# Stick-breaking attention without the weights: running products times differences of values, a second gate in pairs, sums of x from the last scores on

## The chip, the cores and the metric

One core of one Trainium2 chip runs the whole layer in one launch. The metric is the device time of an execution in microseconds; the kernel before takes 768.82 us (median of 3 runs, 767.13 to 770.05). PE is the matrix engine, DVE the vector engine, ACT the scalar engine, POOL the fourth compute engine, SP the queue that starts most DMAs; ACT and POOL can start DMAs too. Everything is float32; a product of matrices is made of three passes of rounded parts ("high" times "high", "high" times "low", "low" times "high").

## The reference

```python
u = x @ w_in + b_in                       # x: (1024, 1024)
q, k, v, z_att, glu_a, glu_b, z_conv, g_att, g_conv = split(u)
# 8 heads of 64: beta[t,s] = sigmoid(q_t.k_s / 8), s < t
# A[t,s] = beta[t,s] * prod_{s<j<t} (1 - beta[t,j]);  att[t] = sum_s A[t,s] v[s]
att_branch  = (att * silu(z_att)) @ w_att_proj
c = causal_depthwise_conv(glu_a * sigmoid(glu_b), conv_w) + conv_b       # 31 taps
conv_branch = (silu(layer_norm(c)) * silu(z_conv)) @ w_conv_proj + b_conv_proj
merged = sigmoid(g_att) * att_branch + sigmoid(g_conv) * conv_branch
out = layer_norm(2 ** 0.25 * x + merged @ w_out)
```

## The kernel before, in words

All engines' instructions are written out by a planner: `Timeline` (L65) keeps a modelled clock for each engine, generators yield their next operation with a priority, and the main loop (L1203) puts on PE, in this order of preference, waiting small products, a step of attention (`Attention.step`, L827), or the next group of a "dense" product (`run_dense`, L307). The result is one fixed order for each engine; at run time an engine takes its instructions strictly in that order and each waits for the semaphores of what it reads or overwrites. Tiles come from pools: 43 blocks of 128x1024 (`blk`), 8 half tiles of 128x512 (`hf`), 8 PSUM banks (`bank`).

The stages, in order of time. First the values, v = x times its weights, for eight blocks of 128 tokens (`vps`, L1145). DVE adds the bias (`vraw`, L1158), ACT rounds (`v`, L1160), DVE takes the rest (L1161), so that each head has 64 columns of high and 64 of low parts. Then attention, with dense products between its steps: queries and keys (`qk_item`), the inputs of the convolution (`glu_item`), the gate z_att (`zatt_item`, L1061), and the first parts P1, P2 of "pairs" (`p12_item`). Attention goes by head and by 256 queries (`Unit`): scores (`zps`, L734, L735), two sigmoids on ACT, f = 1 - beta (L742) and b = beta (L743), a running product of f on DVE (L749, from right to left, started by the unit matrix in `eyez`), the weight b times the next product (L752), transposes on PE (`tps`, L767), rounding (`wth`, `wtl`), and the product with v (`pvps`, L790). High and low halves of that product are added by ACT (L805) and DVE (L806) into `att`. When both heads of an `att` tile are done its gate is computed from PSUM (`ev_zatt`, L430) and the product is kept in DRAM (`keep`).

Then the pairs (`run_pairs`, L1023): two groups of 128 output columns are computed in seven half products P1 to P7 in place of eight, from sums and differences of x (`make_t`, L873) and of the weights (`make_s`). Before, there are ten pairs, for g_att, g_conv and z_conv. While the last pair runs, `split_att` (L456) reads `att` back and rounds it into `ach` and `acl`. Then the two projections (`ev_a`, `ev_c`), the output product (`yps`) and the last layer norm. The convolution's multiplications fill DVE at the lowest priority.

Weights come by SP into `wr`, ACT rounds them into `wh`, and the rest `wl` is made by POOL, DVE, or a DMA of POOL's that adds the weights to their negated rounding (L241, L242).

Of the kernel before, what the change touches and what calls it, by code (L numbers as in the profile page):

```python
# [14 lines left out]
P = 128  # L15
# [19 lines left out]

N_BLK, N_HF, N_RAW, N_SPL = 43, 8, 2, 5

N_F, N_W = 3, 5
# [23 lines left out]
W_LAND = 3000  # L62


class Timeline:  # L65
# [96 lines left out]
def layer_kernel(ctx: ExitStack, tc, xT, x, wv, wd, wa, wc, wo, vec, bv, lng, lnb, cst, out):  # L162
# [70 lines left out]
    def split_weight(wh, wl, r, src, direct, then):  # L233
# [21 lines left out]
    def feed(loads=1 << 30):  # L255
        while True:
# [21 lines left out]
            if i < min(loads, len(pieces)):  # L278
# [99 lines left out]
    za_left = [2] * NC  # L378
# [44 lines left out]
    def silu_pre(ps, ci, name):  # L423
        s = hfp.tile([P, HALF], F32, name="sg" + name, tag="hf")
        yield act(0, s, ps, AF.Sigmoid, bias=vcol(ci))
        yield vstt(0, s, ps, vcol(ci), s, ALU.add, ALU.mult)
        drop("ps")
        return s

    def ev_zatt(p):  # L430
        def f(half, cols, ps):
            def g():
                s = yield from silu_pre(ps, ZATT0 + p, f"za{p}{half}")
                a = att[p][:, cols]
                e = yield vtt(1, a, a, s, ALU.mult)
                drop("hf")
                za_left[p] -= 1
                if za_left[p] == 0:
                    keep(("att", p), att[p])

            tl.spawn(g(), tl.t + 165)
        return f

    def keep(key, src, cols=slice(0, S)):

        if key not in kept:
            kept[key] = dram.tile([P, S], F32, name="_".join(map(str, key)), tag="_".join(map(str, key)))
        nc.sync.dma_start(kept[key][:, cols], src)
        n_kept[key] = n_kept.get(key, 0) + 1

    def back(key, name):
        t = blk(name)
        nc.sync.dma_start(t, kept[key])
        return t

    def split_att(p):  # L456
# [61 lines left out]
    def make_cc(i):  # L518

        while n_kept.get(("c", ZCONV0 + i), 0) < 2:  # L520
            yield tl.now + 200
        z = back(("c", ZCONV0 + i), f"zs{i}")
        yield tl.now + 3500
# [184 lines left out]
    slots = {"f": 0, "w": 0}  # L708

    def alloc_unit(u):  # L710
        n = u.nslots
        ft = [blk(f"f{u.h}{u.m}{i}") for i in range(n)]
        bt = [blk(f"b{u.h}{u.m}{i}") for i in range(n)]
        slots["f"] += n
        slots["w"] += n
        if n == 1:
            u.f = [ft[0][:, 0:HALF], ft[0][:, HALF:S]]
            u.w = [bt[0][:, 0:HALF], bt[0][:, HALF:S]]
        else:
            u.f, u.w = [t[:, :] for t in ft], [t[:, :] for t in bt]  # L720
        for tb in range(2):

            last = P * (2 * u.m + tb + 1) - 1
            nc.gpsimd.memset(u.w[tb][:, last:last + 1], 0.0)
            tl.cost("G", tl.t, 0)

    def emit_z(u):
# [10 lines left out]
        f, w = u.f[tb], u.w[tb]  # L738
        c2 = min(c1, n - 1)

        def g():
            yield act(0, f[:, c0:c1], ps[:, :c1 - c0], AF.Sigmoid, n=c1 - c0, scale=-SCALE)  # L742
            yield act(0, w[:, c0:c2], ps[:, :c2 - c0], AF.Sigmoid, n=c1 - c0, scale=SCALE)  # L743
# [5 lines left out]
            yield ("V", 2, n, lambda: nc.vector.tensor_tensor_scan(  # L749
                f[:, 0:n][:, ::-1], f[:, 0:n][:, ::-1], eyez[:, S - n:S][:, ::-1], 0.0, op0=ALU.mult,  # L750
                op1=ALU.max), {"per": 2.083})
            u.ready[tb] = yield vtt(1, w[:, 0:n - 1], w[:, 0:n - 1], f[:, 1:n], ALU.mult, n)  # L752
            if u.nslots == 2 or u.ready[1 - tb] is not None:
                slots["f"] -= 1
# [3 lines left out]
    def emit_t(u):  # L758
# [22 lines left out]
    def emit_pv(u, i, wh, wl):  # L781
# [13 lines left out]
        if i == 0:  # L795
            p = h // 2
            if att[p] is None:
                att[p] = blk(f"att{p}")
            tmp = hf(f"pvt{h}{m}")
            r0 = (h % 2) * DH  # L800
            dst = att[p][r0:r0 + DH, m * 256:(m + 1) * 256].rearrange("p (b t) -> p b t", b=2)[:, ::-1, :]
            two = lambda ap: ap.rearrange("p (b t) -> p b t", b=2)

            def g():
                yield act(0, tmp[0:DH, 0:256], u.ps[DH:P, 0:256], n=256)  # L805
                yield vtt(0, dst, two(u.ps[0:DH, 0:256]), two(tmp[0:DH, 0:256]), ALU.add, 256)  # L806
                drop("ps")
                drop("hf")
                heads_cnt[h] += 1
                if heads_cnt[h] == 4:  # L810
                    heads_done[p] += 1
                    if all(n == 2 for n in heads_done):
                        flags["att"] = True
                        tl.spawn(make_t(0), tl.now)
                        tl.spawn(make_t(1), tl.now)
# [4 lines left out]
    class Attention:  # L820
# [6 lines left out]
        def step(self):  # L827

            now = tl.t
            if self.pvq and self.pvq[0][0] is not None and self.pvq[0][0] <= now - GUARD and \  # L830
# [3 lines left out]
            if self.zd and live["hf"] <= N_HF - 2 and live["ps"] < 7:  # L834
                u = self.zd[0]
                if all(r is not None and r <= now - GUARD for r in u.ready):
                    self.pvq.append(emit_t(u))
                    if not u.t:
                        self.zd.popleft()
                        slots["w"] -= u.nslots  # L840
                    return True
            if self.cur is None and self.wait:
                u = self.wait[0]
                if qk_ready[u.h] <= now and slots["w"] + u.nslots <= N_W and slots["f"] + u.nslots <= N_F:
                    self.cur = self.wait.popleft()
                    alloc_unit(u)
            if self.cur is not None and live["ps"] < 6:
                emit_z(self.cur)
                if not self.cur.z:
                    self.zd.append(self.cur)  # L850
                    self.cur = None
                return True
# [9 lines left out]
    pairs = [(c, c + 1) for c in (*range(GA0, GA0 + NK, 2), *range(GC0, GC0 + NK, 2), *range(ZCONV0, ZCONV0 + NC, 2))]  # L862
# [5 lines left out]
    t12, t34, first = {}, {}, {}  # L868
    source, split_done = {}, {}
# [3 lines left out]
    def make_t(k):  # L873
# [4 lines left out]
        yield tl.now + 4500  # L878
# [4 lines left out]
        yield vtt(1, b[:, hi_], rb[:, lo_], a[:, hi_], ALU.subtract)  # L883
        for t, r, name in ((t12, a, "ta"), (t34, b, "tb")):
# [4 lines left out]
        if k + 2 < NK // 2:  # L889
# [503 lines left out]
```

## Time and profile before

| what | us |
|---|---|
| median of 3 runs (lowest, highest) | 768.82 (767.13, 770.05) |
| the profiled execution | 767.04 |
| its span, first to last instruction | 765.0 |
| PE, DVE, ACT, POOL busy | 748.2, 651.3, 379.7, 69.5 |
| granted TensorE clock, mean | 0.994 |

The span leaves 2.04 us outside it. A busy time counts a stretch once in which instructions of a group overlap; matmuls overlap, so what one costs is read from the distance of starts and not from its own duration.

### The profile page before, as it was taken

To read this page: it belongs to the slowest core of one execution; us is meant where nothing else is said; L and a number is where in the kernel's file an instruction comes from. 1 tells how busy PE (TensorE), PEld (TensorE's weight loads), DVE (VectorE), ACT (ScalarE), POOL (GpSimd) and SP (SyncE) were. 2 spreads that over 40 slices of the span, in tenths; PEclk is the share of its full clock that TensorE was granted. 3 is DMA by queue.
4 is the path that set the end of the run, shared out by engine and by line. 5 is a ranking of instruction groups with operands and counts; after the bars stand their busy time and mean duration, and the time that the engine had idled before them with its cause. 6 is when DMAs were issued, how large, how long until landed. Compare 5 with 4: busy or idle time off the path is not lost.

```text
span 765.0 us, 10211 instructions
## 1 busy us (share of the span) xinstructions
PE 748.2 (98%) x3622; PEld 625.4 (82%) x3622; DVE 651.3 (85%) x1006; ACT 379.7 (50%) x716; POOL 69.5 (9%) x132
## 2 busy tenths in 40 slices
PE   9999999999999999999999999999998999999995
PEld 7888888788888878888888888877786888888885
DVE  7554999999999999997999999999699859810985
ACT  2149965986388799844524433345472424200100
POOL 3311011101011011101100000000000023000000
PEclk9999999999999999999999999999999999999998
DMA  7525123412432224557725454453347876230052
GB/s 233 184 63 110 35 56 74 92 30 62 103 80 59 57 56 96 125 140 259 207 83 185 146 163 155 139 191 125 126 149 240 317 266 217 79 148 1 0 200 75
DMA packets 43394, 98.01 MB, mean 128 GB/s; under 512 B 4816, under 2 KB 5712, under 8 KB 43344
## 3 DMA queue, kind: packets, MB, share of 16 engines
q1 hardware_dynamic: 36864, 85.77, 33.5%
q0 software_dynamic: 6336, 11.54, 9.4%
q8 instruction: 28, 0.46, 0.3%
q14 instruction: 22, 0.18, 0.1%
q10 hardware_dynamic: 144, 0.07, 0.0%
HBM read 77.95 MB, written 19.40 MB: 127 GB/s over the span
## 4 chain that ended last, share of the span: by engine, by line
PE 58%; DVE 25%; ACT 9%; issue 6%; DMA 2%; SPq 0%; DVEq 0%; ACTq 0%
PE dps L203 11%; PE dps L198 11%; PE dps L199 11%; PE vps L1145 6%; DVE cacc L399 4%; PE yps L209 4%; PE yps L210 4%; PE yps L211 4%; PE pvps L790 3%; PE tps L767 3%; DVE cs L399 2%; DVE wl L396 2%; DVE c L396 2%; DVE cacc L396 2%; DVE u L396 2%
## 5 line engine op out<-in xcount | busy, mean ns | idle before, releaser
L198 PE MATMUL dps<-xh,wh 128*128 128x512 f32 x400 | 157.0, 393 | 0.0
L199 PE MATMUL dps<-xl,wh 128*128 128x512 f32 x400 | 156.0, 390 | 0.0
L203 PE MATMUL dps<-xh,wl 128*128 128x512 f32 x400 | 109.0, 391 | 0.0
L749 DVE TENSOR_TENSOR_SCAN f<-f,eyez 128x896 f32<-128x896 f32 (+3 forms) x64 | 85.0, 1343 | 5.1 <-ACT f L393 5.1
L235 ACT ACTIVATE wh<-wr 128x512 fp32r<-128x512 f32 x84 | 53.3, 634 | 72.4 <-DMA wr<-wv 25.5
L199 PEld LDWEIGHTS dps<-xl,wh 128*128 128x128 f32 x400 | 75.2, 188 | 14.2
L198 PEld LDWEIGHTS dps<-xh,wh 128*128 128x128 f32 x400 | 75.1, 188 | 14.3
L203 PEld LDWEIGHTS dps<-xh,wl 128*128 128x128 f32 x400 | 74.1, 188 | 14.6
L399 DVE SCALAR_TENSOR_TENSOR cacc<-cin,vecs,cacc 128x511 f32<-128x511 f32 (+14 forms) x116 | 82.4, 735 | 0.1
L242 POOL DMA_DIRECT2D wl<-wd x44 | 38.2, 868 | 271.7 <-ACT wl L241 240.8
L239 POOL TENSOR_TENSOR wl<-wr,wh 128x512 fp32r<-128x512 f32 x18 | 26.2, 1460 | 293.9 <-DVE wl L237 231.1
L210 PE MATMUL yps<-wol,mh 128*128 128x512 f32 (+1 forms) x136 | 51.2, 377 | 0.0
L211 PE MATMUL yps<-woh,ml 128*128 128x512 f32 (+1 forms) x136 | 51.2, 376 | 0.0
L209 PE MATMUL yps<-woh,mh 128*128 128x512 f32 (+1 forms) x136 | 51.2, 376 | 0.0
L396 DVE TENSOR_TENSOR wtl<-tps,wth 128x384 fp32r<-128x384 f32 (+1 forms) x80 | 46.7, 625 | 4.0 <-ACT wth L393 3.5
L399 DVE SCALAR_TENSOR_TENSOR xrow<-xrow,yps 128x512 f32<-128x512 f32 (+1 forms) x17 | 10.7, 653 | 43.0 <-PE yps L211 42.7
L393 ACT ACTIVATE f<-zps 128x384 f32<-128x384 f32 (+2 forms) x96 | 45.3, 515 | 3.8 <-PE zps L735 3.0
L393 ACT ACTIVATE wth<-tps 128x384 fp32r<-128x384 f32 (+1 forms) x80 | 40.2, 559 | 13.9 <-PE tps L767 13.2
L396 DVE TENSOR_TENSOR b<-b,f 128x895 f32<-128x895 f32 (+3 forms) x64 | 46.8, 743 | 0.3
L393 ACT ACTIVATE b<-zps 128x383 f32<-128x383 f32 (+2 forms) x96 | 46.2, 536 | 0.1
L399 DVE SCALAR_TENSOR_TENSOR cs<-cs,hs__77 128x511 f32<-128x511 f32 (+14 forms) x60 | 44.1, 735 | 0.1
L790 PE MATMUL pvps<-wtl,v 128*128 128x256 f32 (+1 forms) x160 | 39.7, 287 | 0.3 <-DVE wtl L396 0.2
(174 smaller groups left out, 1637.6 us busy)
## 6 DMA issues: line engine op xcount, KB each, us to landing
wr<-wd SPq DMA_DIRECT2D x60, 256.0 KB, 3.0
wl<-wd POOLq DMA_DIRECT2D x44, 256.0 KB, 4.6
rc<-wd SPq DMA_DIRECT2D x20, 512.0 KB, 5.6
c<-c SPq DMA_DIRECT2D x30, 256.0 KB, 3.1
ga<-c SPq DMA_DIRECT2D x8, 512.0 KB, 5.2
wor<-wo SPq DMA_DIRECT2D x16, 256.0 KB, 4.7
gc<-c SPq DMA_DIRECT2D x8, 512.0 KB, 6.3
xrow<-x SPq DMA_DIRECT2D x8, 512.0 KB, 5.8
```

The lines of the kernel that those rows point to most:

```text
L198: nc.tensor.matmul(ps, wh[:, kk], mh, start=first and kk is ks[0], stop=False)
L199: nc.tensor.matmul(ps, wh[:, kk], ml, start=False, stop=False)
L203: nc.tensor.matmul(ps, wl[:, kk], mh, start=False, stop=last and kk is ks[3])
L209: nc.tensor.matmul(ps, wh, mh, start=first, stop=False)
L210: nc.tensor.matmul(ps, wh, ml, start=False, stop=False)
L211: nc.tensor.matmul(ps, wl, mh, start=False, stop=last)
L235: yield "A", 1, HALF, lambda: nc.scalar.activation(wh, r, AF.Copy)
L393: return "A", u, n, (lambda: nc.scalar.activation(out, in_, func, **kw)), (BIAS if "bias" in kw else {})
L396: return "V", u, n, lambda: nc.vector.tensor_tensor(out, a, b, op=op)
L399: return "V", u, n, (lambda: nc.vector.scalar_tensor_tensor(out, a, s, b, op0, op1)), (PTR if ptr else {})
L749: yield ("V", 2, n, lambda: nc.vector.tensor_tensor_scan(f[:, 0:n][:, ::-1], f[:, 0:n][:, ::-1], eyez[:, S - n:S][:, ::-1], 0.0, op0=ALU.mult,
L790: nc.tensor.matmul(u.ps[:, 0:n], st, wt[:, jj * 256:jj * 256 + n], start=(i == m and jj == 0 and wt is wh), stop=(i == 0 and jj == 1 and w ...
```

## The change

Attention: with R[s] the running product of f from s to the query, a weight is R[s+1] - R[s], so the sum over s of weight times v[s] is v of the token before plus the sum of R[s] times (v[s-1] - v[s]). The second sigmoid, its tile and the multiplication go. For the differences, each block of v is copied one row down by a DMA of 127 rows from ACT's queue, with one more DMA for the row that comes from the block before; DVE subtracts. The leading v is transposed on PE (32 transposes) and copied by ACT into `att`, and each product of attention is then added by two DMAs of POOL's (high half, low half) in place of ACT's and DVE's addition. `pvps` waits until all v are there.

z_att is computed by two more pairs, kept in DRAM, and multiplied in `split_att`, which now reads eight blocks. The order of the dense products is a string; `make_t` starts when the last head's scores are out. DMAs take their turn on one modelled clock (`Timeline.dma`).

```diff
+T_AT = (7, 7)
-N_F, N_W = 3, 5
+N_F = 6
+ORDER = "q0 q1 g0 q2 g1 q3 p2 q4 q5 g2 p2 q6 q7 p2 g3 p3"
-W_LAND = 3000
+DMA_RATE, W_ACC = 250, 2.2
+    def dma(self, kb, when=None, weight=1.0):
+        when = max(self.now, self.t) if when is None else when
+        self.dma_free = max(self.dma_free, when) + weight * kb * 1024 / DMA_RATE
+        return self.dma_free + 2000
...
     def split_att(p):
+        yield from stored(("c", ZATT0 + p))
         a = back(("att", p), f"attb{p}")
-        yield tl.now + 3500
+        z = back(("c", ZATT0 + p), f"zab{p}")
+        yield landed[f"zab{p}"]
...
+            yield vtt(1, a[:, c], a[:, c], z[:, c], ALU.mult)
             yield act(0, ach[p][:, c], a[:, c])
             yield vtt(1, acl[p][:, c], a[:, c], f32(ach[p][:, c]), ALU.subtract)
...
             yield act(0, f[:, c0:c1], ps[:, :c1 - c0], AF.Sigmoid, n=c1 - c0, scale=-SCALE)
-            yield act(0, w[:, c0:c2], ps[:, :c2 - c0], AF.Sigmoid, n=c1 - c0, scale=SCALE)
...
-            u.ready[tb] = yield vtt(1, w[:, 0:n - 1], w[:, 0:n - 1], f[:, 1:n], ALU.mult, n)
...
-                yield act(0, tmp[0:DH, 0:256], u.ps[DH:P, 0:256], n=256)
-                yield vtt(0, dst, two(u.ps[0:DH, 0:256]), two(tmp[0:DH, 0:256]), ALU.add, 256)
+                yield act(0, two(tmp[:, 0:256])[:, ::-1, :], two(u.ps[:, 0:256]), n=256)
                 drop("ps")
+                for part in (slice(0, DH), slice(DH, P)):
+                    e = yield "G", 1, 0, (lambda part=part: nc.gpsimd.dma_start(dst, tmp[part, 0:256],
+                                                                                accum_op=ALU.add)), {"extra": 430}
+                    yield tl.dma(64, e, W_ACC) + 2000
...
-    pairs = [(c, c + 1) for c in (*range(GA0, GA0 + NK, 2), ...
+    pairs = [(c, c + 1) for c in (*range(ZATT0, ZATT0 + NC, 2), *range(GA0, GA0 + NK, 2), ...
...
     def ev_v(tb):
+        vraw[tb] = b = blk(f"vraw{tb}")
+        t, s = b[:, 0:HALF], b[:, HALF:S]
+        yield vtt(0, t, vps[tb], bvt, ALU.add)
+        drop("ps")
+        raw_there.add(tb)
+        while tb and tb - 1 not in raw_there:
             yield tl.now + 100
+        nc.scalar.dma_start(s[1:P, :], t[0:P - 1, :])
+        if tb:
+            nc.scalar.dma_start(s[0:1, :], vraw[tb - 1][P - 1:P, 0:HALF])
+        else:
+            nc.gpsimd.memset(s[0:1, :], 0.0)
+        got = []
+        def turn():
+            ps = bank("tps")
+            for p in range(NC):
+                nc.tensor.transpose(ps[:, p * P:(p + 1) * P], t[:, p * P:(p + 1) * P], ident)
+            tl.t += 4 * 109
+            got.append(ps)
+        yield turn
+        ps = got[0]
+        yield [act(1, att[p][:, tb * P:(tb + 1) * P], ps[:, p * P:(p + 1) * P], n=P) for p in range(NC)]
+        drop("ps")
+        yield tl.now + 1500
         vt[tb] = blk(f"v{tb}", F32R)
...
+        yield vtt(1, s, s, t, ALU.subtract)
+        yield "A", 0, HALF, lambda: nc.scalar.activation(v3[:, :, 0:DH], s3, AF.Copy)
+        yield "V", 1, HALF, lambda: nc.vector.tensor_tensor(v3[:, :, DH:P], s3, f32(v3[:, :, 0:DH]), op=ALU.subtract)
```

ACT's order before, just after the product for v (`vps`): its roundings of v, the weights of the next dense product, then the evacuation of head 0's queries and keys (`qhh`, `qll`, `ks`). What stands in brackets is what an instruction waits for; DMAHW0 to DMAHW7 are the eight marks that DMAs of SP and ACT take in turn.

```order
L1160 ACTIVATE v_458<-vraw_457 128x8x64 [waits DVE_49]
L1160 ACTIVATE v_464<-vraw_463 128x8x64 [waits DVE_49]
L235 ACTIVATE wh_408<-wr_406 128x512 [waits DMAHW7_49,PE_49,Pool_49]
L1160 ACTIVATE v_468<-vraw_467 128x8x64 [waits DVE_49]
L241 ACTIVATE wl_409<-wr_406 128x512
L1160 ACTIVATE v_487<-vraw_486 128x8x64 [waits DVE_49]
L235 ACTIVATE wh_473<-wr_471 128x512 [waits DMAHW0_49,PE_49,Pool_49]
L241 ACTIVATE wl_474<-wr_471 128x512
L393 ACTIVATE qhh_524<-dps,vecs 128x512 [waits PE_49]
```

ACT's order now, at the same place: the DMAs for the fifth to the eighth block of v and the first copies into `att`.

```order
L1146 DMA vraw_461<-vraw_461 127x512 [waits DMAHW0_49,DVE_49]
L1148 DMA vraw_461<-vraw_456 1x16x32 [waits DMAHW1_49]
L252 ACTIVATE wl_409<-wr_406 128x512
L1146 DMA vraw_467<-vraw_467 127x512 [waits DMAHW2_49,DVE_49]
L1148 DMA vraw_467<-vraw_461 1x16x32 [waits DMAHW4_49]
L1146 DMA vraw_472<-vraw_472 127x512 [waits DMAHW5_49,DVE_49]
L1148 DMA vraw_472<-vraw_467 1x16x32 [waits DMAHW6_49]
L1146 DMA vraw_486<-vraw_486 127x512 [waits DMAHW7_49,DVE_49]
L1148 DMA vraw_486<-vraw_472 1x16x32 [waits DMAHW0_49]
L403 ACTIVATE att_442<-tps 128x128 [waits PE_49]
L403 ACTIVATE att_443<-tps 128x128
```

The DMAs of all eight blocks now stand ahead of the copies into `att`, and the later ones wait for marks that the earlier ones hold; by the waits on DVE below, DMAHW0 is the first block's DMA, DMAHW1 the second's, DMAHW6 and DMAHW7 the fourth's.

DVE's order before, from the end of the roundings of v to the first running products (`f`) of head 0.

```order
L1161 TENSOR_TENSOR v_468<-vraw_467,v_468 128x8x64 [waits Activation_49]
L1161 TENSOR_TENSOR v_487<-vraw_486,v_487 128x8x64 [waits Activation_49]
L399 SCALAR_TENSOR_TENSOR qll_525<-dps,vecs,qhh_524 128x512 [waits Activation_49] x2
L749 SCALAR_TENSOR_TENSOR f_605<-f_605,eyez 128x896 [waits Activation_49]
L399 SCALAR_TENSOR_TENSOR qll_643<-dps,vecs,qhh_642 128x512 [waits Activation_49]
L396 TENSOR_TENSOR b_607<-b_607,f_605 128x895 [waits DVE_49]
L749 SCALAR_TENSOR_TENSOR f_606<-f_606,eyez 128x1024
```

DVE's order now, at the same place.

```order
L406 TENSOR_TENSOR vraw_456<-vraw_456 128x512 [waits DMAHW7_49,DMAHW6_49]
L406 TENSOR_TENSOR vraw_461<-vraw_461 128x512 [waits DMAHW1_49,DMAHW0_49]
L406 TENSOR_TENSOR vraw_467<-vraw_467 128x512 [waits DMAHW4_49,DMAHW2_49]
L406 TENSOR_TENSOR vraw_472<-vraw_472 128x512 [waits DMAHW6_49,DMAHW5_49]
L409 SCALAR_TENSOR_TENSOR qll_607<-dps,vecs,qhh_606 128x512 [waits Activation_49]
L406 TENSOR_TENSOR vraw_486<-vraw_486 128x512 [waits DMAHW7_49,DMAHW0_49]
L1171 TENSOR_TENSOR v_620<-vraw_472,v_620 128x8x64 [waits Activation_49]
L1171 TENSOR_TENSOR v_629<-vraw_486,v_629 128x8x64 [waits Activation_49]
L409 SCALAR_TENSOR_TENSOR qll_607<-dps,vecs,qhh_606 128x512 [waits Activation_49]
L736 SCALAR_TENSOR_TENSOR f_700<-f_700,eyez 128x896 [waits Activation_49]
L736 SCALAR_TENSOR_TENSOR f_701<-f_701,eyez 128x1024 [waits Activation_49]
```

The subtractions, each waiting for its block's two DMAs, now stand ahead of head 0's queries and keys (`qll`), and no multiplication stands behind a running product any more.

ACT's order now, a little later: from the rounding of the eighth block of v to the first tiles of head 0's queries and keys (`qhh`, `qll`, `ks`); four more rows stand before the first `f`.

```order
L1170 ACTIVATE v_629<-vraw_486 128x8x64 [waits DMAHW7_49,DMAHW0_49,DVE_49]
L403 ACTIVATE qhh_606<-qhh_606 64x512 [waits Activation_49]
L403 ACTIVATE qll_607<-qll_607 64x512 [waits Activation_49]
L403 ACTIVATE qhh_606<-dps,vecs 128x512 [waits PE_49]
L403 ACTIVATE ks_608<-qhh_606 64x512 [waits Activation_49]
L403 ACTIVATE ks_608<-qll_607 64x512 [waits DVE_49]
```

Head 0's tiles, which PE needs for the first scores, are finished behind the rounding of the last block of v; before, that rounding stood ahead of the first `qhh`.

## Rows read from the trace of the kernel before

**Rows 1.** The page: busy time of each engine (share of the span).

```profile
PE 748.2 (98%) x3622; PEld 625.4 (82%) x3622; DVE 651.3 (85%) x1006; ACT 379.7 (50%) x716; POOL 69.5 (9%) x132
```

**Rows 2.** Busy time by stretch: busy us of each engine, clock, DMA share, GB/s.

```profile
180.00:200.00 20.00, 20.00 (x113) 17.27 (x112) 19.81 (x31) 9.97 (x21) 1.73 (x2) 1.00 0.27 54
...
340.00:360.00 20.00, 20.00 (x90) 16.57 (x89) 15.44 (x23) 9.42 (x14) 1.96 (x3) 1.00 0.85 282
...
580.00:600.00 20.00, 17.48 (x67) 13.31 (x67) 15.56 (x24) 5.46 (x9) 0.00 (x0) 0.91 0.92 326
...
660.00:680.00 20.00, 20.00 (x90) 16.57 (x89) 10.39 (x16) 3.16 (x5) 0.00 (x0) 1.00 0.58 211
```

**Rows 3.** Waits of PE: us in total, times, longest us.

```profile
PE dps L199 <- DVE acl L396: 2.5, 3, 1.0
PE tps L767 <- DVE b L396: 1.6, 4, 0.5
PE sps L203 <- DVE wl L396: 1.3, 1, 1.3
```

**Rows 4.** Waits of PE's weight loads.

```profile
PEld tps L767 <- ACT ks L393: 1.9, 2, 0.9
PEld zps L735 <- ACT qll L393: 1.5, 5, 0.3
...
PEld tps L767 <- DVE b L396: 0.8, 2, 0.6
```

**Rows 5.** The chain in order of time: start us, us, what.

```profile
100.55 1.21 PE tps L767 x11
...
343.21 0.91 PE dps L203 x4
345.93 0.91 PE dps L203 x4
```

**Rows 6.** The page's costliest groups: count, busy us, mean ns, idle before.

```profile
L396 DVE TENSOR_TENSOR b<-b,f 128x895 f32<-128x895 f32 (+3 forms) x64 | 46.8, 743 | 0.3
L393 ACT ACTIVATE b<-zps 128x383 f32<-128x383 f32 (+2 forms) x96 | 46.2, 536 | 0.1
```

**Rows 7.** Groups of DVE and ACT by shape, same columns.

```profile
L396 DVE TENSOR_TENSOR u<-sps,u 128x512 f32<-128x512 f32 x30 | 20.4, 680 | 0.0
...
L396 DVE TENSOR_TENSOR att<-pvps,pvt 64x256 f32<-64x256 f32 x32 | 12.7, 407 | 1.4 <-ACT pvt L393 0.9
...
L393 ACT ACTIVATE qhh<-qhh 64x512 fp32r<-64x512 f32 x16 | 10.1, 631 | 0.4
...
L393 ACT ACTIVATE f<-zps 128x128 f32<-128x128 f32 x8 | 2.6, 320 | 0.0
```

**Rows 8.** The timeline after the product for v: start us, us, what.

```profile
45.01 4.77 DVE L396 TENSOR_TENSOR vraw<-vps,bvt 128x512 f32<-128x512 f32 x7 [12.25 <-PE vps L1145]
...
49.34 0.39 PE L1145 MATMUL vps<-wh,xl 128*128 128x512 f32 x1
...
64.98 0.33 PE L734 MATMUL zps<-ks,qhh 128*128 128x384 f32 x1
```

**Rows 9.** The page's DMA packets, and queues: packets, MB, share of 16 engines.

```profile
DMA packets 43394, 98.01 MB, mean 128 GB/s; under 512 B 4816, under 2 KB 5712, under 8 KB 43344
...
q1 hardware_dynamic: 36864, 85.77, 33.5%
q0 software_dynamic: 6336, 11.54, 9.4%
...
q10 hardware_dynamic: 144, 0.07, 0.0%
```

**Rows 10.** DMA issues: count, KB each, median us from issue to landing.

```profile
wl<-wd POOLq DMA_DIRECT2D x44, 256.0 KB, 4.6
...
p<-p SPq DMA_DIRECT2D x10, 256.0 KB, 3.0
...
attb<-att SPq DMA_DIRECT2D x4, 512.0 KB, 5.7
```

**Rows 11.** The timeline of PE after its waits for `acl`.

```profile
584.67 0.50 PE L199 MATMUL dps<-acl,wh 128*128 128x512 f32 x1 [1.00 <-DVE acl L396]
585.00 1.68 PE L203 MATMUL dps<-ach,wl 128*128 128x512 f32 x4
...
586.91 0.63 PE L199 MATMUL dps<-acl,wh 128*128 128x512 f32 x1
```

More of the change, by code (lines that the diff above doesn't have):

```diff
@@ L421, in ev_qk @@
         return f
[L423 to L442, printed above, removed]
+    landed = {}
     def keep(key, src, cols=slice(0, S)):
@@ L712, in alloc_unit @@
         ft = [blk(f"f{u.h}{u.m}{i}") for i in range(n)]
-        bt = [blk(f"b{u.h}{u.m}{i}") for i in range(n)]
         slots["f"] += n
[L715 to L725, printed above, removed]
+        u.f = [ft[0][:, 0:HALF], ft[0][:, HALF:S]] if n == 1 else [t[:, :] for t in ft]
     def emit_z(u):
@@ L811, in g @@
                     heads_done[p] += 1
+                    if heads_done[p] == 2:
+                        keep(("att", p), att[p])
                     if all(n == 2 for n in heads_done):
                         flags["att"] = True
-                        tl.spawn(make_t(0), tl.now)
-                        tl.spawn(make_t(1), tl.now)
+                        for k in {0, 1} - t_begun:
+                            tl.spawn(make_t(k), tl.now)
                         next_pair()
@@ L829, in step @@
             now = tl.t
-            if self.pvq and self.pvq[0][0] is not None and self.pvq[0][0] <= now - GUARD and \
+            if v_left[0] == 0 and self.pvq and self.pvq[0][0] is not None and self.pvq[0][0] <= now - GUARD and \
                     (self.pvq[0][1].ps is not None or live["ps"] < 7):
@@ L851, in step @@
                     self.cur = None
+                    for k, h in enumerate(T_AT):
+                        if k not in t_begun and heads_z_done(h):
+                            t_begun.add(k)
+                            tl.spawn(make_t(k), tl.t)
                 return True
             return False
-    pairs = [(c, c + 1) for c in (*range(GA0, GA0 + NK, 2), *range(GC0, GC0 + NK, 2), *range(ZCONV0, ZCONV0 + NC, 2))]
+    pairs = [(c, c + 1) for c in (*range(ZATT0, ZATT0 + NC, 2), *range(GA0, GA0 + NK, 2), *range(GC0, GC0 + NK, 2), *range(ZCONV0, ZCONV0 + NC, 2))]
     OPERAND = {"P3": "S4", "P4": "A22", "P5": "S1", "P6": "S2", "P7": "S3"}
@@ L1071, in p12_item @@
         add_item(wd_src(pairs[n][0]), None, ev_p12(n), lambda: True, 1)
[L1073 to L1094 removed]
+    p12 = iter(range(len(pairs)))
+    for what in ORDER.split():
+        if what[0] == "q":
+            qk_item(int(what[1:]))
+        elif what[0] == "g":
+            glu_item(int(what[1:]))
+        else:
+            for _ in range(int(what[1:])):
+                p12_item(next(p12))
+    for n in p12:
         p12_item(n)
@@ L1178, in layer_kernel @@
     v_left = [NT]
+    for p in range(NC):
+        att[p] = blk(f"att{p}")
     for tb in range(NT):
```

94 lines of the change are left out of this document (33 added, 61 removed).

## The prediction

> **What bounds the kernel now.** I read the page's busy times first: PE 98%, DVE 85% of 765.0 us [rows 1]. Then the stretches: in 180 to 200 us PE has all 20.00 us and DVE 19.81; in 340 to 360, 580 to 600 and 660 to 680 DVE is anywhere from 10 to 16 of 20 us while PE stays full but for 17.48 in the second [rows 2]. So PE bounds every stretch, and DVE matters where PE waits for it. The waits of PE say where: 2.5 us for `acl` ahead of the first projection, 1.6 us (and 0.8 more at its weight loads) for the weights `b` of attention, 1.3 us for `wl` in the pairs [rows 3, 4]. Everything else that PE loses is small. The reader is to see that a change can gain here in two ways only, fewer columns on PE or fewer of these few microseconds of waiting, and can lose without limit wherever PE's fixed order meets something late.
>
> The sum is made against the profiled execution, 767.0 us, whose span is 765.0; the median of the runs is 768.8, so I add 1.8 us at the end.
>
> **PE's work.** A half product of 12 matmuls takes 2.72 us (343.21 to 345.93), 0.227 us for one; 11 transposes take 1.21 us, 0.11 each [rows 5]. z_att leaves the dense products (four chunks of 48 matmuls, 192) and comes back as two pairs of seven half products (168): 24 matmuls fewer, -5.4 us. The 32 transposes of v cost +3.5 us. Scores, transposes of attention and products with v keep their counts. PE: -2.0 us.
>
> **DVE and ACT.** DVE loses the 64 multiplications (46.8 us) [rows 6], 32 additions into `att` (12.7) and 16 operations on z_att at about 0.7 (11.4); it gets 16 subtractions and multiplications on full halves and, for two pairs, 40 operations, each at 0.68 like `u` [rows 7], 38 us: some 32 us less. ACT loses 46.2 us of second sigmoids [rows 6] and gets about 12 back. None of this is time by itself, since PE covers it; its worth is what PE waits. With no multiplication behind a running product the waits for `b`, 2.4 us, go [rows 3, 4]: -2.4. What is late next there is the running product itself, which the planner schedules against. The waits for `wl` I halve: -0.7. The waits for ACT's `ks` and `qll` (3.4 us [rows 4]) may shrink with ACT's load; bound -3.4 to 0, I take 0 since they sit in the chain of a head's keys, which does not change.
>
> **The end of the pairs.** `split_att` reads eight blocks of 512 KB instead of four, and each half takes one more multiplication. One such read lands in 5.7 us [rows 10]; the whole, 4 MB at the 326 GB/s of the busiest stretch, takes 13 us [rows 2], beside some 16 us (six half products) between the start of the reads and the end of the pairs. The convolution's norm is out of DVE's way earlier, since its inputs come earlier in the string. Bounds: -5 (the stall for `acl` of 2.5 and the slow clock behind it vanish) and +8 (the last read late); I take 0, the row itself. The clock part is read from the trace: after the third wait for `acl` the matmuls have 0.63 us instead of 0.39 and the granted clock of the stretch is 0.91, so for a few us it was on 1.2 GHz instead of 2.4 [rows 2, 11].
>
> **The additions by DMA.** 64 DMAs of 64 KB from POOL, each pair in sequence. No such transfer stands in the trace; the nearest, 256 KB from the same queue, lands in 4.6 us [rows 10]. While they run they hold half tiles that `wth` and `wtl` need, and `wl` DMAs of the weights queue behind them on POOL. The planner allows over 4.5 us for each. Bounds -1 to +22 (a rival below); I take 0.
>
> **The copy of v, one row down.** This decides the forecast. Eight DMAs of 127 rows of 2 KB stand on ACT's queue. How were transfers dealt to the 16 DMA engines so far? The packets tell: q1 has 36864 for its 256 issues, q0 6336 for 44, ACT's queue 144 for one: always 144, that is 128 rows and 16 small ones. The page's 4816 packets under 512 B are 16 for each of the 301 transfers [rows 9]. So each of the 16 engines got an equal share, eight rows and one closing packet. Every transfer so far had a number of rows that 16 divides. 127 is a prime: no equal shares but one exist. Two ends, then. If the rows are dealt unevenly, the transfer is like the 256 KB ones, 3.0 us to landing [rows 10]. If the share must be equal, all 127 rows go through one engine. In 660 to 680 us the engines moved 211 GB/s at a busy share of 0.58, so 22.7 GB/s each [rows 2]; 260 KB at that rate take 11.4 us, and eight on the same engine 92 us. (The one-row DMAs stand in the order as 16 pieces of 32 numbers; the 127 rows stand undivided.) Between ends so far apart I take the second, because equal shares are what all 301 transfers show, where the 3.0 us is the time of a transfer that has such shares.
>
> The Trainium skill, "DMA: Bandwidth & Descriptors", section on why a DMA increments its semaphore by 16, says just this: the number of engines is the largest up to 16 that divides the slowest dimension on both sides, so 127 partitions go to one, the lowest-numbered. The trace agrees as far as it goes (16 closing packets for every transfer of 128 rows); no run here has one of 127. By the rule the copy costs what follows; without it, what the first rival says.
>
> What it would do: the product for v ends at 49.6 us, its first block's bias is added by 45.7 (seven in 4.77 us from 45.01) [rows 8]. First DMA out at 45.8; with 2 us around a transfer (3.0 less its moving time) they land at 59, 71, 82, 94, 105, 117, 128, 139 us. ACT's queue holds them all ahead of the copies into `att`, and the last of them waits for the fifth's landing, 105 us. Until then PE's next dense product has no bank, because all eight hold transposed v: it stands from about 53 to 106 us. Then it runs 70 matmuls, 15.9 us, to 122, and needs head 0's keys. On DVE the subtraction for the seventh block stands ahead of the first `qll`, on ACT the rounding of the eighth ahead of the last of `qhh` and `qll`; so 139.4, one subtraction (0.68), one rounding (0.62) and nine ACT operations at 0.63 [rows 7]: first scores at 146.4 us. Without any lateness they would be at 49.6 + 3.5 + 15.9 = 69.0 us (before: 65.0 [rows 8]). Lost: 77 us. The cover that hid such things is gone because everything PE could do meanwhile stands behind these scores in its order. Add 2 us for a slow clock after the pause, as after `acl`.
>
> Sum: 767.0 - 2.0 - 2.4 - 0.7 + 77 + 2 = 841; a little faster packets than my average, which counts waiting, would take some 5 us off, and the runs' median adds 1.8: **840 us**. Its own range is 815 to 860.
>
> **Rivals.**
> 1. *The 127 rows are spread over the engines and land like any 256 KB.* For it: 3.0 us for `p` and the like [rows 10]. Against: the equal shares. Then ACT is tight but whole: 32 copies of 128 columns (0.32 us each at most, half of that where they follow each other) and 15 issues push head 0's keys by 1 to 2 us. Time: 767.0 - 2.0 - 2.4 - 0.7 + 1.5 = 763.4, and the waits for ACT may give 1.5 more: 762 to 763, with the 1.8 about 764. Faster, between 755 and 771.
> 2. *Each transfer goes to one engine, but to another one each time.* Then the first four land at 59 to 61 us, the last four, which wait for their marks, at 73, and the scores come at about 80: 11 us lost, 776 with all terms.
> 3. *The additions by DMA come late* (the first rival otherwise). Landing much above 4.5 us would hold half tiles and the weights' DMAs on POOL; at 0.7 us for each of the 32 units (0.5 to 1.0 is the longest of PE's waits [rows 3]) this is +22 us: 785. For it: 64 more transfers on a queue that had 44; against: POOL has 9% of the span [rows 1], and each transfer is a quarter of the known ones.
> 4. *The reads at the end of the pairs decide*: +8, which brings rival 1 to 772, no change.
>
> **How the numbers follow.** Forecast 0.57; rival 1 0.33, rival 2 0.03, rival 3 0.05, rival 4 0.02. A difference under 0.5% (765.0 to 772.7) is about what a measurement of this kernel cannot tell from none. Faster holds most of rival 1: 0.24. Within: the rest of rival 1 and rival 4, 0.09. Slower: 0.67. Both signs hold much of the chance, so the range for 8 in 10 runs from the fast end of rival 1, 757, to the slow end of the forecast, 858.
>
> **What would show it.** Right: in the timeline after the product for v, DMAs of `vraw` with landings some 11 us apart; PE idle from about 53 us and again before the first scores; the granted clock low there; ACT waiting for DMAs; packets of 127 rows with one closing packet, so that packets under 512 B are fewer than 16 for a transfer. Behind that stretch PE nearly full, no wait for `b`, and the rest of the span some 5 us shorter than before. Wrong: first scores near 69 us, the `vraw` DMAs landing in 2 to 4 us; then rival 1 holds and the forecast is wrong by its one large term. If the first scores come near 80 us it is rival 2; if PE's idle time lies at `pvps`, `wth` or dense weights between 70 and 350 us, rival 3.

## The result, and the profile after

The changed kernel takes 836.06 us (median of 4 runs, 835.88 to 837.54) against 767.98 us for the kernel before (now 4 runs); the ratio is 1.0892, 95% interval 1.0856 to 1.0928. Its profiled execution has a span of 834.1 us, 69.1 more than before. The page of after: busy time of each engine (share of the span).

```profile
PE 746.1 (89%) x3630; PEld 624.1 (75%) x3630; DVE 620.6 (74%) x950; ACT 351.8 (42%) x656; POOL 114.1 (14%) x129
```

PE does 2.1 us less work than in [rows 1], DVE 30.7 less, ACT 27.9 less, and yet the span is longer: time was added in which nobody works. The stretches of after say where (busy us of each engine, clock, DMA share, GB/s; columns as in [rows 2]).

```profile
60.00:80.00 20.00, 0.00 (x0) 0.00 (x0) 0.69 (x1) 0.00 (x0) 0.81 (x1) 0.50 0.11 38
80.00:100.00 20.00, 0.00 (x0) 0.00 (x0) 0.69 (x1) 1.26 (x2) 1.02 (x1) 0.50 0.19 50
100.00:120.00 20.00, 0.00 (x0) 0.00 (x0) 0.00 (x0) 0.00 (x0) 0.00 (x0) 0.50 0.07 26
```

For 60 us PE does nothing, the other engines nearly nothing, and the DMA engines are busy at 0.07 to 0.19: one of sixteen is 0.06. PE's timeline of after, around that hole (start us, us, what, idle before).

```profile
49.54 3.65 PE L1157 MATMUL tps<-eyez,vraw 128*128 128x128 f32 x32
125.26 0.80 PE L209 MATMUL dps<-xh,wh 128*128 128x512 f32 x1 [72.06 <-ACT att L403]
125.85 0.63 PE L210 MATMUL dps<-xl,wh 128*128 128x512 f32 x1
126.28 0.63 PE L209 MATMUL dps<-xh,wh 128*128 128x512 f32 x1
...
142.82 0.44 PE L723 MATMUL zps<-ks,qhh 128*128 128x384 f32 x1
144.13 0.44 PE L724 MATMUL zps<-ks,qll 128*128 128x384 f32 x1 [0.86 <-ACT qll L403]
```

The 32 transposes of v end at 53.2 us; the next product waits 72.06 us for a bank, which ACT's copies into `att` free. Behind the pause the first matmuls start 0.43 us apart (125.85 to 126.28) in place of 0.227: the granted clock was 0.50 for 60 us, which is 1.2 GHz. The first scores come at 142.82 us, against 64.98 in [rows 8]. ACT's timeline of after shows what it was doing (ACTq is its sequencer, which starts DMAs).

```profile
45.70 1.86 ACTq L1146 DMA_DIRECT2D vraw<-vraw  x2
47.60 11.09 ACTq L1148 DMA_DIRECT2D vraw<-vraw  x1
...
115.09 9.28 ACTq L1148 DMA_DIRECT2D vraw<-vraw  x1
124.42 3.51 ACT L403 ACTIVATE att<-tps 128x128 f32<-128x128 f32 x20 [32.13 <-issue]
...
143.44 0.63 ACT L403 ACTIVATE qll<-qll 64x512 fp32r<-64x512 f32 x1
```

After two copies of 127 rows have been started, the next DMA on the queue (a single row, L1148) takes 11.09 us to be started, and six more take 9.19 to 10.60 us. DVE's subtractions of after give the landings.

```profile
59.00 0.69 DVE L406 TENSOR_TENSOR vraw<-vraw 128x512 f32<-128x512 f32 x1 [8.57 <-DMA vraw<-vraw]
70.06 0.69 DVE L406 TENSOR_TENSOR vraw<-vraw 128x512 f32<-128x512 f32 x1 [10.37 <-DMA vraw<-vraw]
80.66 0.69 DVE L406 TENSOR_TENSOR vraw<-vraw 128x512 f32<-128x512 f32 x1 [9.90 <-DMA vraw<-vraw]
```

The first three copies land 11.1 and 10.6 us apart, one behind the other. The packets of ACT's queue, on the page of after:

```profile
q10 hardware_dynamic: 1392, 2.16, 0.7%
```

In [rows 9] this queue had 144 packets: 128 rows and 16 closing ones. Now it has 1248 more. The seven one-row DMAs are 16 pieces and 16 closings each, 224; 1024 are left for eight copies, 128 each: 127 rows and one closing packet, so one engine. Behind the scores the total is as forecast. Waits of PE in after (us in total, times, longest us):

```profile
PE dps L209 <- ACT att L403: 72.1, 1, 72.1
PE dps L210 <- DVE acl L406: 3.0, 3, 1.1
PE tps L751 <- DVE f L736: 1.1, 4, 0.4
```

The waits for `b` and `wl` of [rows 3] are gone, 1.1 us for `f` stands in the first one's place, and from the first scores to the end it is 691.3 us (834.1 - 142.8) against 700.0 (765.0 - 65.0).

### The profile page after: what moved, and what is told of

The parts are those of the page before. It is cut to its first block, busy times and chain, and to the rows that moved or that the text cites. A ratio compares the mean times of both kernels' runs of the same rounds, so it can differ in the third digit from the quotient of the medians.

```text
span 834.1 us, 10183 instructions
## 1 busy us (share of the span) xinstructions
PE 746.1 (89%) x3630; PEld 624.1 (75%) x3630; DVE 620.6 (74%) x950; ACT 351.8 (42%) x656; POOL 114.1 (14%) x129
## 4 chain that ended last, share of the span: by engine, by line
PE 65%; DVE 18%; ACTq 8%; DMA 4%; ACT 2%; issue 2%; POOL 0%; SPq 0%; DVEq 0%; POOLq 0%
PE dps L214 8%; PE dps L210 8%; PE dps L209 8%; ACTq L1148 7%; DVE cacc L409 7%; PE sps L209 6%; PE sps L214 6%; PE sps L210 6%; PE vps L1126 5%; PE yps L222 3%; PE yps L221 3%; PE yps L220 3%; PE pvps L774 3%; DVE cs L409 3%; PE tps L751 3%; DVE f L736 2%
## 5 line engine op out<-in xcount | busy, mean ns | idle before, releaser
L209 PE MATMUL dps<-xh,wh 128*128 128x512 f32 x352 | 141.4, 402 | 72.1 <-ACT att L403 72.1
L210 PE MATMUL dps<-xl,wh 128*128 128x512 f32 x352 | 138.2, 393 | 0.0
L209 PEld LDWEIGHTS dps<-xh,wh 128*128 128x128 f32 x352 | 66.7, 189 | 85.1 <-ACT att L403 72.3
L214 PE MATMUL dps<-xh,wl 128*128 128x512 f32 x352 | 99.1, 396 | 0.0
L246 ACT ACTIVATE wh<-wr 128x512 fp32r<-128x512 f32 x80 | 50.9, 639 | 93.1 <-issue 25.2
L210 PEld LDWEIGHTS dps<-xl,wh 128*128 128x128 f32 x352 | 66.8, 190 | 12.7
L214 PEld LDWEIGHTS dps<-xh,wl 128*128 128x128 f32 x352 | 64.2, 188 | 12.0
L791 POOL DMA_DIRECT2D att<-pvt x64 | 55.9, 994 | 91.6 <-ACT pvt L403 61.8
L751 PE MATMUL tps<-eyez,f 128*128 128x128 f32 x288 | 42.4, 275 | 1.1 <-DVE f L736 1.1
L1171 DVE TENSOR_TENSOR v<-vraw,v 128x512 fp32r<-128x512 f32 x8 | 5.4, 686 | 48.6 <-ACT v L1170 48.6
L409 DVE SCALAR_TENSOR_TENSOR xrow<-xrow,yps 128x512 f32<-128x512 f32 (+1 forms) x17 | 10.7, 653 | 41.2 <-PE yps L222 41.0
```

Source lines behind the costliest of these rows:

```text
L209: nc.tensor.matmul(ps, wh[:, kk], mh, start=first and kk is ks[0], stop=False)
L210: nc.tensor.matmul(ps, wh[:, kk], ml, start=False, stop=False)
L214: nc.tensor.matmul(ps, wl[:, kk], mh, start=False, stop=last and kk is ks[3])
L409: return "V", u, n, (lambda: nc.vector.scalar_tensor_tensor(out, a, s, b, op0, op1)), (PTR if ptr else {})
L751: nc.tensor.transpose(ps[:, o:o + P], u.f[tb][:, j * P:(j + 1) * P], ident)
L791: e = yield "G", 1, 0, (lambda part=part: nc.gpsimd.dma_start(dst, tmp[part, 0:256], accum_op=ALU.add)), {"extra": 430}
```

## The experiments

**Rows that divide.** Theory: a copy on this queue is dealt in equal shares, so 127 rows go through one engine. Rival: such a copy is slow, or held, for another reason. Two kernels differ in one row:

```diff
-        nc.scalar.dma_start(s[1:P, :], t[0:P - 1, :])
+        nc.scalar.dma_start(s[1:113, :], t[0:112, :])      # second kernel: 114, 113
+        nc.scalar.dma_start(s[113:P, :], t[112:P - 1, :])
```

> The 127 rows of each block are copied by two DMAs of ACT's queue, 112 rows and 15 rows. Equal shares (the forecast's theory): 112 rows go to 16 engines and 15 rows to 15, so each block's copy lands in about 3 us and the packets of up to 4 bytes number 16 and 15 a transfer instead of 1. ACT's queue then holds 23 issues of some 0.62 us from 45.7 us on, the first copy into att comes near 60.5 us instead of 124.4, PE stands 7 to 8 us instead of 72, first scores at 75 to 79 us instead of 142.8, time 766 to 774. Rival (a copy from SBUF to SBUF on this queue is slow whatever its rows): the same bytes take the same time, 830 to 845.

> As the kernel with 112 and 15 rows, but 113 and 14: the same number of DMAs and bytes, one row moved from one to the other. Equal shares: 113 is a prime, so those rows go through one engine, 113 packets of 84 ns, 9.5 us a block and 76 for eight instead of 85; time 824 to 838. Rival (two smaller transfers instead of one large are what helps): as with 112 and 15, 766 to 774.

112 and 15 rows: 774.69 us, ratio 1.0106 (1.0079 to 1.0133). 113 and 14 rows: 828.25, ratio 1.0806 (1.0764 to 1.0848). One row from one DMA to the other is worth 54 us. The packets of the first kernel agree with equal shares: ACT's queue has 1632 on its page, 240 more than in after, and eight times 31 closing packets (16 and 15) in place of one are 240 more. The first copy into `att` frees PE in the first kernel at 63.85 us; ACT's timeline of it, for one of the eight blocks, and PE's row:

```profile
56.40 0.52 ACTq L1146 DMA_DIRECT2D vraw<-vraw  x1
56.96 0.84 ACTq L1147 DMA_DIRECT2D vraw<-vraw  x1
57.84 0.56 ACTq L1149 DMA_DIRECT2D vraw<-vraw  x1
```

```profile
63.85 0.79 PE L209 MATMUL dps<-xh,wh 128*128 128x512 f32 x1 [10.70 <-ACT att L403]
```

Three issues a block cost about 2.1 us, 17.3 for all (45.65 to 62.96), not the 14.3 I had counted. So PE still stands 10.7 us, and the time is just above my 766 to 774. The equal shares hold; the split is a poor mend, because ACT issues instead of copying.

**The queue.** The same copy of 127 rows, started by POOL, or by SP:

```diff
-        nc.scalar.dma_start(s[1:P, :], t[0:P - 1, :])
+        nc.gpsimd.dma_start(s[1:P, :], t[0:P - 1, :])      # second kernel: nc.sync
```

> The 127 rows of each block stay one DMA, but POOL's queue starts it instead of ACT's. Equal shares for every queue: one engine again, 825 to 845, now with the weights' DMAs of POOL queued behind. If equal shares hold only for the queues of SP and ACT, and POOL's software queue deals rows one by one: landings in about 5 us, ACT has only the seven one-row issues, PE does not stand at all after the transposes of v, first scores near 70 us, time 759 to 766.

> The 127 rows of each block stay one DMA, but SP's queue starts it. If ACT's queue being blocked is the cost (rival), ACT's copies into att come right behind its one-row DMAs, PE does not stand before 100 us, time 762 to 785. If one engine carrying all rows is the cost (forecast's theory): the last blocks of v still land 85 us after the first start, head 0's keys and the products with v are held by the roundings on ACT and DVE, and SP's weights queue behind the same engine: 815 to 850.

From POOL: 761.79 us, ratio 0.9938 (0.9917 to 0.996), a little faster than before. From SP: 837.47, ratio 1.0926 (1.0883 to 1.097). DMA issues of the kernel with POOL's copies (count, KB each, median us to landing), from 45 to 150 us, and PE's first scores:

```profile
vraw<-vraw POOLq DMA_DIRECT2D x8, 254.0 KB, 5.6
```

```profile
69.44 0.44 PE L723 MATMUL zps<-ks,qhh 128*128 128x384 f32 x1 [0.38 <-ACT qhh L403]
```

On POOL's queue the same 127 rows land in 5.6 us with eight close together, and the scores come at 69.4 us: the forecast's 69.0 for a kernel without lateness. That kernel is the change without its hole; 836.06 - 761.79 = 74.3 us is the price of the hole. With SP ACT's queue has only the single rows, and it helps nothing. Waits of PE in SP's kernel:

```profile
PE dps L209 <- ACT att L403: 39.3, 1, 39.3
PE dps L214 <- DMA wl<-wd: 22.1, 1, 22.1
```

The loss is spread, but it is of the same size. SP's queue is now held as ACT's was, up to 10.06 us for one issue, and with it the loads of weights (`wr`) that stand on it. ACT's and POOL's timelines of that kernel:

```profile
124.76 0.63 ACT L246 ACTIVATE wh<-wr 128x512 fp32r<-128x512 f32 x1 [17.82 <-DMA wr<-wd]
127.56 1.86 POOL L253 DMA_DIRECT2D wl<-wd  x2 [74.65 <-ACT v L1170]
```

So `wl` is 22 us late because POOL starts it only at 127.56, behind ACT, which stood 17.82 us for weights of SP's; the transfer itself has landed by 134.22, when PE goes on. This run shows that the loss does not hang on ACT's queue. That both queues fill the same engine, it does not show; the next program does.

**The cost by itself.** A program with nothing but copies of n rows, each waited for by DVE.

```diff
+    def one(q, n):
+        o = 0 if n == P else 1
+        q.dma_start(dst[o:o + n, :], src[0:n, :])
+        nc.vector.tensor_copy(sink, dst)
...
+    for n in (128, 127, 126, 125, 124, 122, 120, 119, 113, 112, 64, 16, 15):
+        one(nc.scalar, n)
...
```

> Leaves out the whole layer: only copies of n rows of 2 KB inside SBUF, one after another, each waited for (its output is x itself). Equal shares over the largest number of engines up to 16 that divides n, 84 ns for a row on one engine, and some 2 us around it: 128 rows 2.7 us to landing, 127 rows 12.7, 126 (14 engines) 2.8, 125 (5) 4.1, 124 (4) 4.6, 122 (2) 7.1, 120 (15) 2.7, 119 (7) 3.4, 113 (1) 11.5, 112 (16) 2.6; on SP's queue the same; on POOL's queue 127 and 100 rows like 128. Rival (time by bytes): all from 112 to 128 rows within 0.4 us of each other. Two copies of 127 rows started together: if the engine is always the same, the second lands some 10.7 us behind the first, also when one is ACT's and one SP's; if the engines change, both after 12.7. Six of 127 rows on ACT: the third issue and those behind it are held until an earlier one has landed; six of 112 rows are issued without a pause, 0.6 us each.

DVE's timeline of that program; what stands in brackets is the issue and the landing of one copy. First 128, 127, 126 and 125 rows, then 120, 119 and 113; then 127 rows from SP and from POOL; then two copies of 127 started together on ACT, and two on ACT and SP.

```profile
6.62 0.43 DVE L189 COPY sink<-one 128x512 f32<-128x512 f32 x1 [2.46 <-DMA one<-src]
20.26 0.43 DVE L189 COPY sink<-one 128x512 f32<-128x512 f32 x1 [13.21 <-DMA one<-src]
23.92 0.43 DVE L189 COPY sink<-one 128x512 f32<-128x512 f32 x1 [3.23 <-DMA one<-src]
29.02 0.43 DVE L189 COPY sink<-one 128x512 f32<-128x512 f32 x1 [4.66 <-DMA one<-src]
...
47.05 0.43 DVE L189 COPY sink<-one 128x512 f32<-128x512 f32 x1 [3.23 <-DMA one<-src]
51.81 0.43 DVE L189 COPY sink<-one 128x512 f32<-128x512 f32 x1 [4.33 <-DMA one<-src]
64.26 0.43 DVE L189 COPY sink<-one 128x512 f32<-128x512 f32 x1 [12.02 <-DMA one<-src]
...
91.95 0.43 DVE L189 COPY sink<-one 128x512 f32<-128x512 f32 x1 [13.15 <-DMA one<-src]
...
98.73 0.43 DVE L189 COPY sink<-one 128x512 f32<-128x512 f32 x1 [3.13 <-DMA one<-src]
...
115.97 0.43 DVE L205 COPY sink<-twoa 128x512 f32<-128x512 f32 x1 [12.88 <-DMA twoa<-src]
126.14 0.43 DVE L205 COPY sink<-twob 128x512 f32<-128x512 f32 x1 [9.74 <-DMA twob<-src]
...
148.17 0.43 DVE L205 COPY sink<-mixa 128x512 f32<-128x512 f32 x1 [20.94 <-DMA mixa<-src]
150.68 0.43 DVE L205 COPY sink<-mixb 128x512 f32<-128x512 f32 x1 [2.08 <-DMA mixb<-src]
```

Time follows the rows of one engine, not the bytes: 127 rows (one engine) 13.21 us, 126 (14 engines, 9 rows each) 3.23, 125 (5, 25 rows) 4.66, 119 (7, 17 rows) 4.33, 113 (one) 12.02. From 113 to 127 rows it is 1.19 us for 14 rows, 85 ns a row. 124 and 122 rows took 5.81 and 7.72; my 4.6 and 7.1, and most of my other figures for fewer than 16 engines, were 0.4 to 1.2 too low. Two copies on ACT land 10.2 us apart, and one on ACT with one on SP needs 21 us and more for both (a load of SP's stood behind them): the engine is the same one for both queues. That rules out the rival in which each copy goes to another engine. The packets agree with equal shares: ACT's queue has 3359 on that program's page, of which 3126 are rows, and the 233 left are just the closing packets of the engines that equal shares give to its 28 copies.

The program ends with six copies of 127 rows started together on ACT, and then six of 112:

```profile
152.17 7.41 ACTq L203 DMA_DIRECT2D sixb<-src  x1
...
159.68 11.76 ACTq L203 DMA_DIRECT2D sixc<-src  x1
...
167.69 0.43 DVE L205 COPY sink<-sixa 128x512 f32<-128x512 f32 x1 [14.57 <-DMA sixa<-src]
```

The third issue ends at 171.44, after the first copy has landed, and the three behind it take 10.14 to 10.76 us. The second, which I had not expected to be held, takes 7.41 us here and 4.37 in the pair of copies before. The issues of 112 rows take 0.55 to 0.95 us each.

**A copy that nobody reads.** Into the kernel before, at the place where a block of v has its bias:

```diff
+        nc.scalar.dma_start(blk(f"dum{tb}")[1:128, 0:HALF], eyez[0:127, 0:HALF])   # second kernel: 112 rows
```

> The kernel before, and at the place where each block of v has its bias, ACT starts a copy of 127 rows of 2 KB into a tile that nobody reads. Forecast's theory, with the queue held as in the run of single copies (at most about two of 127 rows under way): ACT's roundings of v and the queries and keys of head 0 stand behind the copies, ACT comes free when the sixth or seventh has landed, 110 to 122 us, and PE stands 40 to 60 us: 800 to 830. Rival (only a reader of the copied rows pays): eight issues of 0.6 us, 766 to 773.

> The same with 112 rows in place of 127, so 16 engines in place of one and 12% fewer bytes. Forecast's theory: eight issues of 0.6 us on ACT, no more, 766 to 773. Rival (extra transfers of this size at this place cost by their bytes): as with 127 rows, 800 to 830.

127 rows: 820.26 us, ratio 1.0687 (1.0655 to 1.0719). 112 rows: 768.98, ratio 1.0015 (1.0001 to 1.003). ACT's timeline of the kernel with 127 rows:

```profile
45.54 0.61 ACTq L1160 DMA_DIRECT2D dum<-eyez  x1
...
46.34 1.28 ACTq L1160 DMA_DIRECT2D dum<-eyez  x1
...
47.68 12.06 ACTq L1160 DMA_DIRECT2D dum<-eyez  x1
59.79 0.63 ACT L1161 ACTIVATE v<-vraw 128x512 fp32r<-128x512 f32 x1 [11.49 <-issue]
```

The third copy is held until 59.74, 14.2 us after the first was started (13.21 is what one takes alone), and ACT's own work behind it with it. The last hold ends at 102.4, earlier than the 110 to 122 I had expected. So some 52 us of the hole are paid without a reader, through the queue and the shared engine alone. What the other 22 are, the readers or the transposes' banks, was not measured.

**The other parts, on the kernel with POOL's copy.** First the additions, back on ACT (two copies of 64 rows in place of one of 128) and DVE:

```diff
-                yield act(0, two(tmp[:, 0:256])[:, ::-1, :], two(u.ps[:, 0:256]), n=256)
+                for i in range(2):
+                    yield act(0, two(tmp[r, i * 256:i * 256 + 256])[:, ::-1, :], two(u.ps[i * DH:i * DH + DH, 0:256]), n=256)
...
-                for part in (slice(0, DH), slice(DH, P)):
-                    e = yield "G", 1, 0, (lambda part=part: nc.gpsimd.dma_start(dst, tmp[part, 0:256],
...
+                for i in range(2):
+                    yield vtt(0, dst, dst, tmp[r, i * 256:i * 256 + 256], ALU.add, 256)
```

> The kernel with POOL's copy of v, but each product of attention is added to att by ACT (two copies of 64 rows) and DVE (two additions) in place of two accumulating DMAs of POOL's. DVE gets 64 additions of 0.41 us, 26 us, ACT some 12 us more, POOL's queue 64 DMAs less. Forecast's theory (the DMAs cost nothing, and DVE's busy time is covered by PE): within 0.5% of the copy by POOL, 758 to 766. Rival 1 (the DMAs hold half tiles and POOL's queue): faster, 754 to 758. Rival 2 (DVE is short in attention, so its 26 us come out as waits of PE for f and wtl): 766 to 775.

770.94 us, ratio 1.0053 (1.0034 to 1.0072) against 0.9938 with the DMAs: 9.1 us more. Pages of the kernel with DMAs, then with additions:

```profile
PE 744.1 (98%) x3630; PEld 623.0 (82%) x3630; DVE 620.3 (82%) x950; ACT 351.5 (46%) x656; POOL 118.8 (16%) x137
```

```profile
PE 749.6 (97%) x3630; PEld 625.2 (81%) x3630; DVE 645.4 (84%) x1014; ACT 364.8 (47%) x688; POOL 66.0 (9%) x73
```

25 us more of DVE and 13 more of ACT cost 9 us of time, so "PE covers it" is wrong in attention. Which of the two engines costs it, this run does not separate: the waits of PE's weight loads for `wtl`, which DVE writes, grow from 1.3 to 4.6 us; the rest is spread, and I did not trace it. (This is not the addition of before, which wrote `att` once per product; here `att` already holds the leading v.) Then the gate back in dense products, with `ev_zatt` as before and ten pairs:

```diff
-ORDER = "q0 q1 g0 q2 g1 q3 p2 q4 q5 g2 p2 q6 q7 p2 g3 p3"
+ORDER = "q0 q1 g0 q2 g1 q3 z0 q4 q5 g2 z1 q6 q7 p2 z2 g3 p1 z3"
...
```

> The kernel with POOL's copy of v, but z_att is computed by dense products in attention as before, multiplied into att there, and the pairs are ten again. Forecast's theory: 24 matmuls more, 5.4 us; four reads fewer at the end of the pairs take back some of the 4.5 us that PE waits for acl: 763 to 768. Rival (the second gate's place in the pairs costs as much as it saves): 759 to 763.

767.93 us, ratio 1.0016 (1.0 to 1.0031): 6.1 us more than with the gate in pairs, where 24 matmuls are 5.4 by the forecast's 0.227 us for one. No wait for `acl` is left in it, so the pairs lose that much at their end and still win.

**A better version.** With POOL's copy PE waits 3.0 us for `acl`. The split of `att` was started earlier and put first on DVE; then the reads of the convolution's gate (`zs`) were taken from SP to POOL.

```diff
-        att_at = {"P5": (0,), "P6": (1, 2, 3)}
+        att_at = {("P5", n2): (0,), ("P5", n2 + 1): (1,), ("P6", n2 + 1): (2, 3)}
...
-        nc.sync.dma_start(t, kept[key])
+        (nc.gpsimd if name.startswith("zs") else nc.sync).dma_start(t, kept[key])    # second kernel only
```

> The kernel with POOL's copy of v, and the split of att at the end of the pairs starts two half products earlier for one block and one earlier for another, its multiplications and subtractions ahead of other work on DVE. If the 3.0 to 4.5 us that PE waits for acl are DVE's order: they go, 756 to 759. If the reads' landing decides, or the tiles they take hold the last pairs: 760 to 764.

> As the kernel with the earlier split of att, but the four reads of the convolution's gate (zs) are started by POOL's queue, which has nothing to do there, in place of SP's. If the 5.5 us that PE waited for wh at 600 us came from the weights of the projection standing behind these reads on SP: they go, and 755 to 759 are left. If the weights are late for another reason (buffers, the order of the DMA marks): 762 to 766, as with the earlier split alone.

The first alone: 764.65 us, ratio 0.9973 (0.9956 to 0.9989), by its middle slower than without it, though the intervals touch. The wait for `acl` is gone, and another stands in its place: 5.5 us for the weights `wh` of the projection. SP's timeline before it:

```profile
590.64 0.38 SPq L439 DMA_DIRECT2D c<-c  x1
594.84 0.32 SPq L445 DMA_DIRECT2D zs<-c  x1
...
596.20 0.38 SPq L295 DMA_DIRECT2D wr<-wa  x1
```

The read of `zs` waits 4 us for the store of the same data to land, and the projection's weights `wr` stand behind it. With `zs` on POOL: 760.27 us, ratio 0.9906 (0.9886 to 0.9926), by its middle the fastest of all; that wait is then 1.6 us. Against the version with POOL's copy alone (761.79) the intervals overlap; the spans of the profiled executions are 758.4 and 760.1.

## Why the prediction was right

**The copy of v.** Forecast 840 us (its sum with both corrections is 838), measured 836.06. The step that decided held: one engine, always the same, one copy behind the other. Forecast: landings 11.4 us apart and scores at 146.4, 77 us later than without lateness, and 2 us for the clock. Measured: landings 11.1 and 10.6 us apart in after and 10.2 in the program of copies; scores at 142.8, 73.4 later than in the kernel with POOL's copy (69.4), the slow clock within that. The transfers were a little faster than I had them: I had taken 22.7 GB/s from a stretch whose busy share counts waiting too; 85 ns for 2 KB are 24 GB/s.

**A step that failed, and came out near by luck.** I let the last DMA wait for the fifth copy's mark, so that ACT would be free at 105 us and PE stand until 106; the scores would then wait for the landing of the eighth copy. ACT came free at 124.4, and PE stood until 125.3: the queue does not take a further DMA while two such copies are under way, whatever the marks say. The scores did not wait for the eighth copy either: its subtraction, the last of the eight, starts at 135.40 and names no wait for a DMA (the rows below). They waited for ACT, which worked from 124.42 to 144.07 with hardly a pause on what stood behind its held queue, head 0's last tile (`qll`) at the end, which I had at 146.4. PE's dense run ends at 142.8 (125.26 and 70 matmuls, the first of them slow), so both chains meet there. So the path to the scores was another than forecast, and its end lies near because two errors met: ACT came free 19 us later than I had it, and the copies landed earlier, the eighth by 135.4 in place of 139. With a longer dense run between the pause and the scores, more of the 19 us would show; no run has that.

```profile
134.80 0.68 DVE L1171 TENSOR_TENSOR v<-vraw,v 128x512 fp32r<-128x512 f32 x1
135.40 0.69 DVE L406 TENSOR_TENSOR vraw<-vraw 128x512 f32<-128x512 f32 x1
```

**PE, the waits and the rest.** Forecast from the first scores on: 5.4 + 2.4 + 0.7 = 8.5 us less. Measured: 8.7, but the sum fits better than its terms. PE's busy time there is 8.0 us shorter (684.9 before, 676.9 after) and its idle time 0.7 us shorter. Its waits with a releaser's name sum to 6.2 us before and to 6.2 after: those for `b` and `wl` went, others for `f`, `acl` and `qll` came. Of the 8.0, the 24 matmuls are 5.4, and some 1.6 are a slow clock behind `acl`: before, nine matmuls there take 3.6 us in place of 2.0 (585.00 to 588.62, clock 0.83 in 580 to 590 us), after has none (1.00 in 650 to 660 us). The rest was not traced.

**The end of the pairs.** Taken at 0 between -5 and +8: PE waits 3.0 us for `acl` instead of 2.5, but stays on the full clock there. So the reads are no trap; another order of DVE and SP there gained 1.5 us by its middle, within the intervals.

**The additions by DMA.** Taken at 0 between -1 and +22. The page of after, in its DMA issues (count, KB each, median us to landing):

```profile
att<-pvt POOLq DMA_DIRECT2D x64, 64.0 KB, 2.9
```

They land in 2.9 us, not the 4.6 of the nearest row [rows 10], and no wait of PE names them. What I got wrong is the worth of the time that they save on DVE and ACT: I called it nothing, and putting such additions back cost 9.1 us.

**The rivals.** The first (rows spread) has the right price, 764 against 761.79, for a queue that spreads them. The second falls with the two copies started together, the third with the 2.9 us, the fourth with the 3.0 us for `acl`.

The rule of the Trainium skill ("DMA: Bandwidth & Descriptors", section on why a DMA increments its semaphore by 16) gave the same as the equal shares: 127 rows one engine, 126 fourteen, 125 five, 119 seven. The trace agrees (13.21, 3.23, 4.66, 4.33 us). The same section has an exception for some copies of POOL's queue, which puts 127 partitions on all 16; the trace agrees with that too (3.13 us).

## What to carry to other kernels

Before a copy is moved to a DMA, look at its number of rows: a queue of SP or ACT uses only as many engines, up to 16, as divide it, and 127 rows cost 13.2 us where 126 or 128 cost about 3. Start it from POOL or, second best here by 13 us, split it; and ask what stands behind it on the queue, because a held issue holds its engine's arithmetic too. A stage in which the bounding engine shows 98% can still pay for other engines' time: 25 us of DVE and 13 of ACT were worth 9 here.

## What was not expected of the hardware

- A queue holds its next DMA while two transfers on a single engine are under way: 11.09 and 10.60 us for one issue in after, 12.06 in the copies that nobody reads. With one such transfer under way the next issue took 1.28 us in the copies that nobody reads, 4.37 and 7.41 in the program of copies. Which resource runs out, no run shows.
- A copy on fewer than 16 engines costs more than its rows: 120 rows on 15 engines, 8 rows each, 3.23 us; 128 rows on 16, also 8 each, 2.46.
- An issue of ACT's takes 0.52 us for 112 rows and 0.84 for 15, more for the smaller one.
